# A hybrid decoder block on one core: two groups of GpSimd subtractions and additions are done on VectorE

## The chip, the cores and the metric

The kernel runs on one core of one Trainium2 chip. Its time is in device microseconds (us), as the median of several executions; smaller is better. A core has five engines that work side by side, each through its own queue in a fixed order: TensorE (PE: matmuls, with its weight loads shown as PEld), VectorE (DVE), ScalarE (ACT), GpSimd (POOL) and SyncE (SP, which here only issues DMAs). They wait for each other by semaphores.

## The reference

One decoder layer over a sequence of 2048 positions, 1024 wide, in float32. A conditioning vector c gives shifts, scales and gates (by a product with `ada_w`). Three groups of mixers share one input projection and one output projection:

```
h = rmsnorm(x, norm1_g) * (1 + sc1) + sh1
p = h @ w_in
y = concat[rglru(p), hgrn2(p), rwkv7(p)] * mix_beta
x = x + g1 * (y @ w_out)
h = rmsnorm(x, norm2_g) * (1 + sc2) + sh2
x = x + g2 * ((silu(h @ w_gate) * (h @ w_up)) @ w_down)
return rmsnorm(x, final_g)
```

RG-LRU and its convolution are scans over time, HGRN-2 a gated linear recurrence worked in chunks of 64, RWKV-7 a delta-rule recurrence. The FFN is 2816 wide.

## The kernel before

Everything lies transposed: channels on the 128 partitions, time along the free dimension. Time is cut into four blocks of 512 (`NB`, `TB`), so a tile is 128x512; the 1024 channels are eight tiles (`KC`).

**Split products.** The large ("dense") products keep float32 accuracy with three passes over split numbers: each operand is a high part (rounded by ACT to the narrower type `R`) and a low part (the rest, by a subtraction). `project` (the line L271 in the profile) issues hi·hi, hi·lo and lo·hi into a PSUM bank `pd`, of which there are three. Weights come through `raw_w` into `wr` (three buffers), are split into `wh` and `wl` (four buffers each), and activations into `hh` and `hl` (sixteen each). There are two helpers for the split of an activation: `split_v`, whose subtraction is on VectorE, and `split`, whose subtraction is on GpSimd (L240).

**Stages.** First the shifts and scales, the norm of block 0, then `w_in` products for two blocks at a time, whose results go to DRAM (`pd`). The mixers read them back (`load_p`), work tile by tile, and store `y` to DRAM (`yd`). When a block's mixers are done, `load_y(b)` reads its eight y tiles into `xs` tiles (12 buffers, shared with the residual x and others), splits each with `split`, and `w_out_products` and `ffn` follow. `load_y` of the next block is called inside `ffn`, ahead of the last group of `w_down` products. So there are four places where `split` works: ahead of blocks 0, 1, 2 and 3. I call them the boundaries.

**Squares of a norm.** `square_sum` adds up the squares of eight x tiles: ACT squares, and the sums are made on VectorE, except where the caller gives tiles of its own (`tile`): that is the norm of block 1, worked out ahead in the start of the kernel with `tr` and `th` tiles, whose six additions are on GpSimd (L344). After `rstd_of` its result waits for `norm1(1)`.

**Mixers beside dense work.** The mixers are generators (`mixers_a`: RWKV; `mixers_b`: HGRN and RG-LRU), stepped by `tick` from within `project`, and so their instructions are mixed into those of the dense products. The names to know: `hgrn` works on `th` tiles, multiplies them on VectorE in six levels (blocks of 1, 2, 4, 8, 16, 32 positions), with products on PE between them into the bank `ph`. Those of the last two levels are the small products of 16x16 and 32x32, which the profile names `ph<-th 64*16` and `64*32`. The VectorE products on `big` tiles (128x126, 128x119 and so on) belong to the mixers' work as well.

**What sets the order.** The program is written through a framework that builds each engine's queue: it takes the instructions that are ready in a model of the run, in which each instruction has an assumed duration, and among those the one with the lowest number. `level` gives the numbers: `out` before `load` (weights), `feed` (activations, and what this change touches), `mix` (mixers), `dense` (matmuls). The order that comes out is fixed; at run time an engine never takes a later instruction first. A helper class `Counted` wraps VectorE and ScalarE, so that nearly all of their instructions have one line in the profile, L69; tile names tell them apart.

Of the kernel before, what the change touches and what calls it, by code (L numbers as in the profile page):

```python
# [10 lines left out]
F = mybir.dt.float32  # L11
# [63 lines left out]
def hybrid_kernel(ctx, tc, x, par, ada_w, w_in, rgw, igw, w_up, a_up, g_up, w_out,  # L75
                  w_gate, w_upf, w_down, cst, msk, out):
    nc = tc.nc
    G, PE, SP = nc.gpsimd, nc.tensor, nc.sync
    V, A = Counted(nc.vector, 0.16, 960.0), Counted(nc.scalar, 0.2, 1200.0)
# [21 lines left out]
    def act(o, i, f=AF.Copy, **k):  # L101
        return A.activation(o, i, f, **k)
# [35 lines left out]
    def parts_():  # L138
        return dp.tile([128, TB], R, name="hh", bufs=16), dp.tile([128, TB], R, name="hl", bufs=16)
# [95 lines left out]
                               lambda: bank("pd", 3), xs_)  # L235


    def split(src, hi, lo):
        act(hi, src)
        G.tensor_sub(lo, src, hi.bitcast(F))  # L240

    def split_v(src, hi, lo):
        i = act(hi, src)
        V.tensor_sub(lo, src, hi.bitcast(F))
        return i
# [48 lines left out]
    def finish(b):  # L294
        for s in streams:
            while s["block"] <= b:
                step(s)
# [39 lines left out]
    def square_sum(s, t, k, tile=None, n=1):  # L337

        s, *last = s or (None,)
        if len(last) == n:  # L340
            if s is None:
                s = last.pop(0)
            else:
                (G if tile else V).tensor_add(s, s, last.pop(0))  # L344
        q = (tile or xs_)()
        if k == KC - 1:
            V.tensor_mul(q, t, t)
        else:
            squared[:] = [act(q, t, AF.Square)]
        return s, *last, q  # L350
# [18 lines left out]
    def load_x(src, b, k, tile=None):  # L369
        t = (tile or xs_)()  # L370
        load(t, src[k, :, b * TB:(b + 1) * TB])
        return t

    def x_stats(bs, step, xtile=None, qtile=None, parts=None):
        for b in bs:
            s = None
            for k in range(KC):
                with level("feed"):
                    t = load_x(x, b, k, xtile)
                    if xtile is not None:  # L380
                        X[b, k] = t
                    s = square_sum(s, t, k, qtile)
                if k % step == step - 1:
                    yield
            with level("feed"):
                RS[b] = rstd_of(s, parts)
# [31 lines left out]
    with level("feed"):  # L418
        xsum = None
        xt = [load_x(x, 0, k) for k in range(KC)]  # L420
        w_after[:] = last_load
        tiles = {}
        for k in range(KC):
            for part, tile in ((1, tr_), (0, th_)):
                tiles[part, 0, k] = ada_tile(tile(), part, 0, k)
        for k in range(KC):
            for part, tag in ((1, "hh"), (0, "hl")):
                tiles[part, 1, k] = ada_tile(dp.tile([128, TB], F, name=tag, bufs=16), part, 1, k)
        for k in range(KC):
            xsum = square_sum(xsum, xt[k], k)  # L430
        rs = rstd_of(xsum)

        def shift_and_scale(half, pe):
            drain(zip_longest(*(ada(part, half, lambda k, part=part: tiles[part, half, k], pm_, xs_, pe)
                                for part in (1, 0))))

        shift_and_scale(0, (0, 2, 4))
        head = IN_ORDER[:2]
        W = {c: load_w(w_in[c], split_v) for c in head}
        w_after[:] = last_load  # L440
        h0 = make_h(lambda k: xt[k], rs, A1, B1, ks=range(4))
        ahead = x_stats([1], 8, tr_, th_, lambda: (tile_of("th", R)[:, 0:TB], tile_of("th", R)[:, 0:TB]))
        next(ahead)
        shift_and_scale(1, (0, 1))
        h0 += make_h(lambda k: xt[k], rs, A1, B1, ks=range(4, KC))
# [593 lines left out]
    for f in (mixers_a, mixers_b):  # L1039
        s = {"block": 0, "at": 0.0}  # L1040
# [3 lines left out]
    def load_y(b):  # L1044
        finish(b)
        ys = []
        for k in range(KC):
            t = load_x(yd, b, k)
            y = parts_()
            split(t, *y)  # L1050
            ys.append(y)
        return ys

    def w_out_products(b, ys, before):
        x1, s = [], None
        for d in range(KC):
            ws = load_w(w_out[d], split_v)
            t = load_x(x, b, d)
            p, = project(ys, ws)
            with level("out"):  # L1060
                stt(t, p, G1[:, d:d + 1], t, OP.mult, OP.add)
            if d == 0:
                before()
            s = square_sum(s, t, d)
            x1.append(t)
        return x1, rstd_of(s)
# [17 lines left out]
    def ffn(b, x1, rs):  # L1084
        h = make_h(lambda k: x1[k], rs, A2, B2, "silu_and_others", over=False)
        gs, s, ys = [], None, None
        for f0 in range(0, NF, 4):
            n = min(4, NF - f0)
            while len(gs) < min(f0 + n + (2 if f0 + n + 2 >= NF else 1), NF):
                gs.append(ffn_up(h, len(gs)))  # L1090
            if len(gs) == NF and ys is None and b + 1 < NB:
                ys = load_y(b + 1)
            for d in range(KC):
                p, = project(gs[f0:f0 + n], load_w(w_down[d][:, f0 * 128:(f0 + n) * 128], split_v))
                with level("out"):
                    stt(x1[d], p, G2[:, d:d + 1], x1[d], OP.mult, OP.add)
                if f0 + n == NF:
                    s = square_sum(s, x1[d], d, n=1 if b + 1 < NB else 2)

        def final_norm():  # L1100
            rs = rstd_of(s)
            for d in range(KC):
                with level("dense"):
                    stt(x1[d], x1[d], pc("final_g", d), rs, OP.mult, OP.mult)
                    SP.dma_start(out[d, :, b * TB:(b + 1) * TB], x1[d])

        return ys, final_norm
# [22 lines left out]
    with level("feed"):  # L1130
        ys, before = load_y(0), lambda: None
# [60 lines left out]
```

## Time and profile before

| what | value |
|---|---|
| median of 3 runs | 2862.96 us (2861.45 to 2866.43) |
| the profiled execution | 2862.48 us |
| its span, first to last instruction | 2860.7 us |
| mean granted clock of TensorE | 0.983 |
| dense products (L271) | 9696 of 14842 matmuls |
| GpSimd's subtractions (L240) | 32, at 866, 1350, 1895 and 2401 us |
| GpSimd's additions (L344) | 6, at 43 to 58 us |
| GpSimd's other work | memsets, 24 of them of KG tiles (22.7 us) |

How to read the rows of a profile: `out<-in` names the tile written and the tiles read, with buffer numbers left out. In a list of groups there follow the shape, the number of instructions, then busy us and mean ns of one, then how long the engine was idle just before them and for whom it waited. In a timeline a row begins with its start and its length in us; the square bracket at its end is the idle time ahead of it. In a list of waits the numbers are us in total, times, and the longest. Granted clock 1.00 is TensorE's full speed.

### The profile page before, as it was taken

The page shows a single profiled execution, that of the slowest core. Times are in us where ns is not written, and L with a number is a line of the kernel's source. Part 1 is how long each engine was busy: PE and PEld are TensorE (multiplying, and loading weights), DVE is VectorE, ACT ScalarE, POOL GpSimd, SP SyncE. Part 2 cuts the span into 40 slices and gives each one's busy share as a digit, 9 for nine tenths or more (in the row PEclk, how much of TensorE's full clock was granted, in tenths as well). Part 3 has the DMA queues.
Part 4 walks back from the last instruction along what each step waited for, and adds up shares of the span by engine and source line. Part 5 has one row for each costly group of instructions (what it writes and reads, how often), then busy time and mean ns, then how long its engine had stood idle before and what let it go on. Part 6 is the DMA issues. An engine that isn't in the chain of part 4 may idle for free. (4 is left out here: it accounts for less than half of the span.)

```text
span 2860.7 us, 41286 instructions
## 1 busy us (share of the span) xinstructions
PE 2732.2 (96%) x14842; PEld 2196.6 (77%) x14842; DVE 1932.6 (68%) x4112; ACT 1476.4 (52%) x2466; POOL 80.0 (3%) x67
## 2 busy tenths in 40 slices
PE   7999998999998999999989999999999999999998
PEld 6787776777876688877767877877778788788886
DVE  7677667867686875687877858778776445644435
ACT  4433854464547743666477456746773433433333
POOL 2000000000001000001000000010000001000000
PEclk9999999999999999999999999999999999999999
DMA  7553455544444242434333434335233333433332
GB/s 256 186 148 114 137 166 161 160 137 145 128 128 131 93 122 81 141 100 137 108 111 97 122 89 129 113 111 158 75 112 102 93 96 121 145 99 96 97 99 85
DMA packets 242590, 352.27 MB, mean 123 GB/s; under 512 B 72913, under 2 KB 78545, under 8 KB 242385
## 3 DMA queue, kind: packets, MB, share of 16 engines
q1 hardware_dynamic: 160144, 285.55, 31.9%
q10 hardware_dynamic: 82240, 64.09, 8.5%
q8 instruction: 117, 1.92, 0.3%
q14 instruction: 89, 0.72, 0.1%
HBM read 293.92 MB, written 55.62 MB: 122 GB/s over the span
## 5 line engine op out<-in xcount | busy, mean ns | idle before, releaser
L271 PE MATMUL pd<-hh,wh 128*128 128x512 f32 x3232 | 1295.1, 402 | 26.7 <-ACT hh L69 23.2
L271 PE MATMUL pd<-hl,wh 128*128 128x512 f32 x3232 | 1284.6, 398 | 5.0 <-DVE hl L69 3.9
L271 PE MATMUL pd<-hh,wl 128*128 128x512 f32 x3232 | 1282.4, 397 | 1.3 <-DVE wl L69 1.3
L69 ACT ACTIVATE wh<-wr 128x512 fp32r<-128x512 f32 (+1 forms) x752 | 464.0, 620 | 892.8 <-PE pd L271 719.6
L271 PEld LDWEIGHTS pd<-hh,wh 128*128 128x128 f32 x3232 | 613.5, 190 | 154.8 <-ACT hh L69 26.2
L271 PEld LDWEIGHTS pd<-hl,wh 128*128 128x128 f32 x3232 | 613.8, 190 | 136.2 <-DVE hl L69 8.9
L69 DVE TENSOR_TENSOR wl<-wr,wh 128x512 fp32r<-128x512 f32 (+1 forms) x752 | 510.8, 683 | 300.9 <-ACT wh L69 282.0
L271 PEld LDWEIGHTS pd<-hh,wl 128*128 128x128 f32 x3232 | 613.4, 190 | 130.3 <-issue 3.3
L69 ACT ACT_TABLE_LOAD x227 | 291.2, 1283 | 9.1 <-DVE tr L69 2.3
L69 DVE SCALAR_TENSOR_TENSOR xs<-pd,Q,xs 128x512 f32<-128x512 f32 x224 | 167.7, 748 | 141.6 <-PE pd L271 132.8
L69 DVE TENSOR_TENSOR th<-th 128x256 f32<-128x256 f32 (+8 forms) x349 | 155.0, 458 | 29.7 <-ACT th L69 23.3
L69 DVE TENSOR_TENSOR big<-big 128x30 f32<-128x30 f32 (+7 forms) x480 | 117.1, 244 | 10.2
L69 DVE TENSOR_TENSOR xs<-pd,xs 128x512 f32<-128x512 f32 x88 | 60.8, 691 | 87.2 <-PE pd L271 85.3
L69 ACT ACTIVATE xs<-pd 128x512 f32<-128x512 f32 x140 | 82.6, 590 | 69.4 <-PE pd L271 61.5
L69 ACT ACTIVATE th<-th 128x512 f32<-128x512 f32 (+2 forms) x153 | 93.3, 611 | 45.5 <-DVE th L69 25.8
L69 ACT ACTIVATE hh<-xs 128x512 fp32r<-128x512 f32 x120 | 74.4, 628 | 40.4 <-DVE xs L69 24.9
L69 ACT ACTIVATE hw<-big,we 64x64 f32<-64x64 f32 x192 | 66.1, 344 | 46.0 <-DVE big L69 43.1
L69 ACT ACTIVATE tr<-tr 128x512 fp32r<-128x512 f32 (+4 forms) x112 | 69.2, 626 | 13.9 <-DVE tr L69 12.9
L240 POOL TENSOR_TENSOR hl<-xs,hh 128x512 fp32r<-128x512 f32 x32 | 43.2, 1377 | 989.2 <-ACT hh L69 987.5
L69 DVE SCALAR_TENSOR_TENSOR big<-pc,we,hw 64x64 f32<-64x64 f32 x168 | 47.4, 282 | 32.5 <-PE pc L302 28.6
L69 DVE TENSOR_TENSOR tr<-tr 128x512 fp32r<-128x512 f32 (+2 forms) x80 | 54.7, 686 | 18.3 <-ACT tr L69 17.8
L69 DVE TENSOR_TENSOR hl<-xs,hh 128x512 fp32r<-128x512 f32 x88 | 60.7, 689 | 6.2 <-ACT hh L69 2.0
(185 smaller groups left out, 2290.7 us busy)
## 6 DMA issues: line engine op xcount, KB each, us to landing
wr<-in_w_gate SPq DMA_DIRECT2D x176, 256.0 KB, 2.6
wr<-in_w_upf SPq DMA_DIRECT2D x176, 256.0 KB, 2.6
wr<-in_w_down SPq DMA_DIRECT2D x160, 256.0 KB, 2.7
wr<-in_w_in SPq DMA_DIRECT2D x144, 256.0 KB, 3.4
pd<-xs SPq DMA_DIRECT2D x108, 256.0 KB, 3.1
xs<-in_x SPq DMA_DIRECT2D x72, 256.0 KB, 4.2
wr<-in_ada_w SPq DMA_DIRECT2D x64, 256.0 KB, 3.3
th<-pd ACTq DMA_DIRECT2D x64, 256.0 KB, 3.5
```

The source lines that it names most:

```text
L69: return f(*a, **k)
L240: G.tensor_sub(lo, src, hi.bitcast(F))
L271: PE.matmul(p, a[:, c], b, start=(n == 0), stop=(n == tot - 1))
```

## The change

The subtraction of `load_y` and the additions in block 1's sum of squares go from GpSimd to VectorE. `split` has no other user and is removed.

```
-    def split(src, hi, lo):
-        act(hi, src)
-        G.tensor_sub(lo, src, hi.bitcast(F))
-
     def split_v(src, hi, lo):
         i = act(hi, src)
         V.tensor_sub(lo, src, hi.bitcast(F))
...
             if s is None:
                 s = last.pop(0)
             else:
-                (G if tile else V).tensor_add(s, s, last.pop(0))
+                V.tensor_add(s, s, last.pop(0))
...
             t = load_x(yd, b, k)
             y = parts_()
-            split(t, *y)
+            split_v(t, *y)
             ys.append(y)
```

Since the queues are built by a model of the run, the order of the other instructions changes as well. GpSimd is left with memsets. VectorE's queue in the start, around the last four x tiles of block 0 (`xs<-xs,Q,rstd` is the norm, `hl<-xs,Q,hh` the low part that PE waits for, `th<-th` an addition of squares), before:

```order
L69 SCALAR_TENSOR_TENSOR xs<-xs,Q,rstd 128x512 x3
L69 TENSOR_TENSOR wl<-wr,wh 128x512 x2
L69 SCALAR_TENSOR_TENSOR xs<-xs,Q,rstd 128x512
L69 COPY tr<-pcar 128x1
L69 SCALAR_TENSOR_TENSOR hl<-xs,Q,hh 128x512 x3
L69 TENSOR_TENSOR th<-tr 128x512
L69 SCALAR_TENSOR_TENSOR hl<-xs,Q,hh 128x512
```

and now:

```order
L69 SCALAR_TENSOR_TENSOR xs<-xs,Q,rstd 128x512 x3
L69 TENSOR_TENSOR wl<-wr,wh 128x512 x2
L69 TENSOR_TENSOR th<-th 128x512
L69 SCALAR_TENSOR_TENSOR xs<-xs,Q,rstd 128x512
L69 TENSOR_TENSOR th<-th 128x512
L69 SCALAR_TENSOR_TENSOR hl<-xs,Q,hh 128x512
L69 TENSOR_TENSOR th<-th 128x512
L69 SCALAR_TENSOR_TENSOR hl<-xs,Q,hh 128x512
L69 TENSOR_TENSOR th<-th 128x512
L69 TENSOR_TENSOR th<-tr 128x512
L69 TENSOR_TENSOR th<-th 128x512
L69 SCALAR_TENSOR_TENSOR hl<-xs,Q,hh 128x512
```

The additions now stand between the low parts: two of them are ahead of the first.

VectorE's queue at the boundary of block 1, around the last `w_down` products of block 0's FFN (`xs<-pd,Q,xs` adds a product to the residual and frees its bank, `wl<-wr,wh` is a weight's low part, `hl<-xs,hh` a subtraction: the first one is the FFN's own, the others are y's; `big` is mixers' work), before:

```order
L69 TENSOR_TENSOR hl<-xs,hh 128x512
L69 TENSOR_TENSOR big<-big 128x6x19
L69 COPY_PREDICATED big<-M,ph 64x32x8
L69 SCALAR_TENSOR_TENSOR xs<-pd,Q_79,xs 128x512
L69 TENSOR_TENSOR big<-big 128x126
L69 TENSOR_TENSOR wl<-wr,wh 128x512
L69 TENSOR_TENSOR big<-big 128x7x18
L69 TENSOR_TENSOR th<-th 128x32x8
L69 TENSOR_TENSOR big<-big 128x119
```

and now:

```order
L69 TENSOR_TENSOR hl<-xs,hh 128x512 x2
L69 SCALAR_TENSOR_TENSOR xs<-pd,Q_79,xs 128x512
L69 TENSOR_TENSOR hl<-xs,hh 128x512
L69 TENSOR_TENSOR wl<-wr,wh 128x512
L69 TENSOR_TENSOR hl<-xs,hh 128x512
L69 TENSOR_TENSOR big<-big 128x6x19
L69 SCALAR_TENSOR_TENSOR xs<-pd,Q_79,xs 128x512
L69 TENSOR_TENSOR wl<-wr,wh 128x512
L69 TENSOR_TENSOR hl<-xs,hh 128x512 x3
L69 SCALAR_TENSOR_TENSOR xs<-pd,Q_79,xs 128x512
L69 TENSOR_TENSOR wl<-wr,wh 128x512
L69 TENSOR_TENSOR hl<-xs,hh 128x512
```

The eight subtractions of y stand among the weights and the residual's additions, and the mixers' `big` and `th` work that was there stands behind them. On PE the products of that work are later by as much: counted in dense products (L271), HGRN's 16x16 step stands 40 later than before and its 32x32 step 33. At the boundary of block 2 the same happens, by 59 and 56 products.

More of the change, by code (lines that the diff above doesn't have):

```diff
@@ L235, in ada_rest @@
                                lambda: bank("pd", 3), xs_)
-    def split(src, hi, lo):
-        act(hi, src)
-        G.tensor_sub(lo, src, hi.bitcast(F))
     def split_v(src, hi, lo):
@@ L343, in square_sum @@
             else:
-                (G if tile else V).tensor_add(s, s, last.pop(0))
+                V.tensor_add(s, s, last.pop(0))
         q = (tile or xs_)()
@@ L1049, in load_y @@
             y = parts_()
-            split(t, *y)
+            split_v(t, *y)
             ys.append(y)
```

## The prediction

> **What bounds the kernel now.** I read the page's head first: how long, and which engine is full.
>
> ```profile
> span 2860.7 us, 41286 instructions
> PE 2732.2 (96%) x14842; PEld 2196.6 (77%) x14842; DVE 1932.6 (68%) x4112; ACT 1476.4 (52%) x2466; POOL 80.0 (3%) x67
> ```
>
> TensorE is the bound: 96% of the span is matmul work that the change leaves alone. Only the other 128.5 us (2860.7 - 2732.2), in which PE idles, can move, and the work that PE does at a reduced clock. A time saved on VectorE (DVE) or GpSimd (POOL) counts only where PE waits for it. So I read next what POOL does and what the same operation costs on DVE, in the view that groups instructions by line (busy us, then mean ns of one).
>
> ```profile
> L240 POOL TENSOR_TENSOR hl<-xs,hh 128x512 fp32r<-128x512 f32 x32 | 43.2, 1377 | 989.2 <-ACT hh L69 987.5 <-DMA xs<-yd 0.8 <-PE pd L271 0.7
> L344 POOL TENSOR_TENSOR th<-th 128x512 f32<-128x512 f32 x6 | 10.3, 1720 | 39.5 <-DMA tr<-in_x 34.6 <-ACT th L69 4.5
> L69 DVE TENSOR_TENSOR hl<-xs,hh 128x512 fp32r<-128x512 f32 x88 | 60.7, 689 | 6.2 <-ACT hh L69 2.0
> L69 DVE TENSOR_TENSOR th<-th 128x512 f32<-128x512 f32 x64 | 43.9, 688 | 16.6 <-ACT th L69 15.9
> ```
>
> The 38 instructions take 53.5 us on POOL. On DVE they cost 38 x 0.69 = 26.2 us: about half each, but on an engine that is 68% busy instead of 3%.
>
> Next, how busy the engines are in the stretches in which POOL does them (columns: stretch, length, then busy us of PE, PEld, DVE, ACT, POOL, then the granted clock).
>
> ```profile
> 49.82:58.03 8.21, 5.69 (x13) 4.05 (x14) 8.21 (x7) 4.39 (x8) 7.89 (x5) 0.58 0.75 223
> 866.45:876.86 10.41, 9.39 (x43) 7.26 (x43) 3.83 (x8) 9.25 (x21) 10.41 (x8) 0.84 0.50 187
> 1349.82:1362.82 13.00, 9.78 (x104) 7.54 (x102) 12.61 (x19) 6.26 (x11) 10.60 (x8) 1.00 0.51 147
> 1894.98:1906.65 11.67, 5.81 (x54) 4.63 (x52) 11.42 (x18) 5.12 (x9) 10.72 (x8) 0.90 0.52 158
> ```
>
> In the start and at the boundaries of blocks 1 and 2, DVE is full while POOL works, and PE is not: 5.81 of 11.67 us in the last row. What fills DVE there? Grouping DVE's instructions in the block 1 stretch, the block 2 stretch, and a stretch just ahead of the first, in that order:
>
> ```profile
> L69 DVE TENSOR_TENSOR wl<-wr,wh 128x512 fp32r<-128x512 f32 x2 | 2.8, 1379 | 0.0
> L69 DVE TENSOR_TENSOR big<-big 128x126 f32<-128x126 f32 x3 | 2.6, 875 | 0.0
> L69 DVE TENSOR_TENSOR big<-big 128x119 f32<-128x119 f32 x2 | 2.6, 1305 | 0.0
> L69 DVE TENSOR_TENSOR big<-big 128x128 f32<-128x128 f32 x2 | 1.6, 823 | 0.1
> L69 DVE SCALAR_TENSOR_TENSOR xs<-pd,Q,xs 128x512 f32<-128x512 f32 x2 | 1.5, 752 | 0.2
> ...
> L69 DVE TENSOR_TENSOR wl<-wr,wh 128x512 fp32r<-128x512 f32 x2 | 2.3, 1150 | 0.0
> L69 DVE TENSOR_TENSOR big<-big 128x128 f32<-128x128 f32 x2 | 2.3, 1136 | 0.0
> L69 DVE TENSOR_TENSOR big<-big 128x119 f32<-128x119 f32 x2 | 2.0, 992 | 0.0
> L69 DVE TENSOR_TENSOR th<-th 128x256 f32<-128x256 f32 x2 | 1.9, 945 | 0.0
> L69 DVE TENSOR_TENSOR big<-big 128x126 f32<-128x126 f32 x2 | 1.2, 615 | 0.0
> ...
> L69 DVE TENSOR_TENSOR wl<-wr,wh 128x512 fp32r<-128x512 f32 x5 | 3.4, 689 | 1.0 <-ACT wh L69 1.0
> L69 DVE TENSOR_TENSOR th<-th 128x256 f32<-128x256 f32 x10 | 4.1, 416 | 0.0
> L69 DVE TENSOR_TENSOR big<-big 128x120 f32<-128x120 f32 x2 | 0.6, 284 | 0.0
> ```
>
> The same instructions last two to four and a half times as long while POOL works. It hits those with two operands in SBUF; the one that reads a PSUM bank (xs<-pd) keeps its 0.75 us. DVE is not short of work capacity there: part of its "busy" time is being held by POOL. Against the third group (big taken at 0.28), block 1 loses 2 x 0.69 + 3 x 0.59 + 2 x 1.02 + 2 x 0.54 = 6.3 us, block 2 2 x 0.46 + 2 x 0.85 + 2 x 0.71 + 2 x 0.53 + 2 x 0.33 = 5.8 us. The start shows it too, on the instructions that PE needs first (one, then three, of a kind that takes 0.75):
>
> ```profile
> 50.07 1.75 DVE L69 SCALAR_TENSOR_TENSOR xs<-xs,Q,rstd 128x512 f32<-128x512 f32 x1
> 51.81 5.08 DVE L69 SCALAR_TENSOR_TENSOR hl<-xs,Q,hh 128x512 fp32r<-128x512 f32 x3
> ```
>
> **What PE pays for it.** PE's rows at those places, with the idle time ahead of each and its releaser, and the list of waits:
>
> ```profile
> 53.56 0.80 PE L271 MATMUL pd<-hl,wh 128*128 128x512 f32 x1 [0.96 <-DVE hl L69]
> 1354.98 0.68 PE L302 MATMUL ph<-th 64*16 64x16 f32 x64 [2.19 <-DVE th L69]
> 1366.38 1.06 PE L302 MATMUL ph<-th 64*32 64x32 f32 x32 [4.60 <-DVE th L69]
> 1905.55 1.07 PE L302 MATMUL ph<-th 64*32 64x32 f32 x32 [5.86 <-DVE th L69]
> PE pd L271 <- POOL hl L240: 1.1, 2, 0.7
> ```
>
> POOL itself holds PE for 1.1 us only. Its larger price goes by way of DVE: HGRN's chain on big and th is late, and PE, whose order is fixed, stands at the product that needs it. After the two long waits PE also runs slowly (first and last slow product after each; then an undisturbed stretch of the chain of waits):
>
> ```profile
> 1367.96 0.63 PE L271 MATMUL pd<-hl,wh 128*128 128x512 f32 x1
> 1371.37 0.57 PE L271 MATMUL pd<-hh,wh 128*128 128x512 f32 x1
> 1907.14 0.63 PE L271 MATMUL pd<-hh,wh 128*128 128x512 f32 x1
> 1910.55 0.63 PE L271 MATMUL pd<-hh,wl 128*128 128x512 f32 x1
> 2240.50 195.88 PE pd L271 x864
> ```
>
> Eight products lie between each pair: 3.41 / 8 = 0.426 us each, against 195.88 / 864 = 0.227. That is 8 x 0.20 = 1.6 us lost after each long wait, 3.2 in all.
>
> **The change, part by part.**
>
> *The subtractions at the boundaries of blocks 1 and 2.* Eight subtractions cost DVE 8 x 0.69 = 5.5 us; the stretching that ends gives back 6.3 and 5.8. For DVE it is a draw. But in the new order PE's products have moved: counting PE's dense products (L271) in it, the 16x16 step of HGRN stands 40 of them later than before in block 1 and 59 in block 2, the 32x32 step 33 and 56 later. The order now counts those subtractions on DVE, while the old one knew nothing of DVE being held. At 0.227 us the slack is 9.1 and 7.5 us in block 1, 13.4 and 12.7 in block 2.
>
> What could eat it: DVE keeps its order, and a subtraction that waits for its y tile holds the queue. Before, only ScalarE (ACT) waited for those tiles:
>
> ```profile
> ACT hh L69 <- DMA xs<-yd: 14.3, 12, 2.6
> SPq L164 <- POOL hl L240: 8.6, 10, 0.9
> ```
>
> That is 14.3 / 4 = 3.6 us a boundary. Bounds for what DVE will wait: 0, since the loads themselves waited 8.6 us for POOL to free a tile, which DVE does in half the time, and 3.6. At 3.6 the chain is later by 5.5 - 6.3 + 3.6 = 2.8 us in block 1 and by 5.5 - 5.8 + 3.6 = 3.3 in block 2. The waits would then be 2.19 + 2.8 - 9.1, 4.60 + 2.8 - 7.5 and 5.86 + 3.3 - 12.7: all at or below zero. So I take all three as gone: **-12.7 us** (2.19 + 4.60 + 5.86), and the slow clock with them, **-3.2 us**. What is late next there is nothing of this chain; it is ACT's weights, whose waits are for PE.
>
> *Block 0's boundary.* DVE is busy 3.83 of 10.41 us; eight subtractions of 0.69 fit in the gaps. PE's 1.1 us of waits on POOL go: **-1.1** (bounds 0 and -1.1). *Block 3's boundary:* nothing, since PE is full and DVE has room:
>
> ```profile
> 2401.26:2412.79 11.53, 11.53 (x52) 9.55 (x52) 7.85 (x9) 6.23 (x12) 11.49 (x8) 1.00 0.56 173
> ```
>
> *The six additions of block 1's squares, in the start.* They stand in DVE's queue between the last xs and the hl that PE waits for: two of them ahead of the first hl. From 50.07: 0.69 + 0.75 + 0.69 + 0.75 ends near 52.95; before, 1.75 and a third of 5.08 end near 53.5. So **-0.5** (bounds: -0.96, the whole wait, and +0.8, if the end of the stretching gives nothing on these).
>
> *The rest of the order.* From about 1350 us to the last mixer's work, PE, DVE and ACT get a different order, the mixers' products mostly 10 to 80 dense products later. No dense product waits for those mixers soon; but the new order has waits of its own. I bound them by 0 and by all that I took off, 17.5. The nearest row is the stretch between the two boundaries:
>
> ```profile
> 1370.00:1893.00 523.00, 508.88 (x2885) 403.63 (x2888) 395.40 (x880) 325.72 (x540) 5.68 (x6) 0.99 0.39 114
> ```
>
> PE idles 14.1 us there. I take half of that as new waits: **+7** (a choice).
>
> **Sum.** -12.7 - 3.2 - 1.1 - 0.5 + 7 = -10.5. The profiled execution took 2862.48 us (1.8 more than its span), the median is 2862.96; so 2852.0 against the one and 2852.5 against the other. I say 2852.
>
> **Rivals.**
>
> *Given back.* The mixers' order is new over 800 us, and every wait removed comes back elsewhere: the 14.1 us of idle above shows that such waits are common outside the POOL stretches too. Then 2862 +- 5. For it: DVE's own balance is a draw (+26.2, less some 16 of stretching). Against: the three waits lie right in the POOL stretches or behind them.
>
> *The queue behind a late y tile (slower).* DVE holds at a subtraction; behind it stand the low parts of weights (wl) and the additions that free PSUM banks; PE stops. Price: ACT's 14.3 us go to PE in full, the old waits stay, less 1.6 for block 0 and the start: 2862.5 + 14.3 - 1.6 = 2875. It decides when one wait outlasts the weights prepared ahead.
>
> ```profile
> ACT wh L69 <- PE pd L271: 719.6, 426, 10.0
> ```
>
> Against it: ACT mostly waits for PE to free a weight tile, up to 10.0 us, so weights are ahead by far more than the longest single wait, 2.6.
>
> *DVE becomes the bound.* If the long instructions above were long for another reason, the 12.61 of 13.00 and 11.42 of 11.67 us stay and 5.5 us come on top in each of the two stretches: 2862.5 + 11.0 = 2873.5. It decides if wl still takes over 1 us there. Against it: the rows ahead of the stretch, and xs<-pd, unchanged inside it. [...]
>
> That the change doesn't do what it says can be left out: POOL's new order holds memsets alone.
>
> **Chances.** Forecast 0.60; given back 0.25; the late tile 0.09; DVE the bound 0.06. About 0.2%, 5.7 us, is what a measurement of this kernel can tell from no change. So faster 0.60, same 0.25, slower 0.15. Range: at the low end the sum with no new waits gives 2845, and 2842 leaves room for a better order; at the high end it takes in all of "given back" and goes to 2869; the two slow cases and a little of the low end are left out.
>
> **What would show it.** Right: wl and big near 0.69 and 0.28 us at the boundaries; no PE wait over 1 us on th at the 16x16 and 32x32 steps of blocks 1 and 2; DVE busy some 5 to 10 us more in all. Wrong: DVE's hl waiting on ACT's hh for several us at a boundary with PE idle behind it; or PE's idle total still near 128.5 us, with new waits on DVE between 1370 and 2240 us.

## The result, and the profile after

The changed kernel took 2846.66 us (median of 6 runs, 2840.93 to 2848.35), the kernel before beside it 2862.53 (6 runs, 2860.56 to 2866.43): ratio 0.9939, 95% interval 0.9926 to 0.9951, so 0.5 to 0.7% faster. The forecast was 2852, with a range from 2842 to 2869.

The head of the page after, and PE's row:

```profile
span 2840.7 us, 41245 instructions
PE 2724.8 (96%) x14842; PEld 2188.8 (77%) x14842; DVE 1934.6 (68%) x4150; ACT 1472.7 (52%) x2464; POOL 26.5 (1%) x29
```

Two differences are to be seen. PE's idle time is the span less PE's busy time: 115.9 us now, 128.5 before, so 12.6 less. And DVE, which got 38 instructions more (26.2 us at 0.69), is busy only 2.0 us longer: some 24 us of what it did before was being held.

In the changed kernel's rows `project` is L267 and the helper of the mixers' products L298; before, they were L271 and L302. DVE's groups in 1346 to 1363 us, the new place of block 1's boundary (busy us, mean ns, idle before):

```profile
L69 DVE TENSOR_TENSOR hl<-xs,hh 128x512 fp32r<-128x512 f32 x9 | 6.0, 685 | 1.2 <-ACT hh L69 1.2
...
L69 DVE TENSOR_TENSOR wl<-wr,wh 128x512 fp32r<-128x512 f32 x4 | 2.7, 685 | 0.5 <-ACT wh L69 0.5
...
L69 DVE TENSOR_TENSOR big<-big 128x126 f32<-128x126 f32 x2 | 0.6, 283 | 0.0
...
L69 DVE TENSOR_TENSOR big<-big 128x119 f32<-128x119 f32 x2 | 0.5, 270 | 0.0
```

`wl` is at 685 ns, where it was 1379, and `big` at 283 and 270, where it was 875 and 1305. The eight subtractions are there and cost 0.69 each. PE's rows at the 16x16 and 32x32 steps of HGRN, block 1 and then block 2, in its timeline:

```profile
1360.37 0.68 PE L298 MATMUL ph<-th 64*16 64x16 f32 x64 [1.67 <-DVE th L69]
...
1366.17 0.70 PE L298 MATMUL ph<-th 64*32 64x32 f32 x32 [0.57 <-DVE th L69]
...
1893.85 0.68 PE L298 MATMUL ph<-th 64*16 64x16 f32 x64 [1.70 <-DVE th L69]
```

Block 1's waits of 2.19 and 4.60 us have become 1.67 and 0.57. Block 2's wait of 5.86 us, at the 32x32 step, is gone, and its 16x16 step, for which PE did not wait before, now has one of 1.70. At these steps PE idled 12.65 us before and 3.94 now: 8.7 less, beside 12.6 in the whole run. Another 4.1 went at a place that the prediction does not name, the second norm of block 1. The rows there, of before:

```profile
1468.41 0.95 PE L302 MATMUL pc<-rs,GIQ 128*128 128x64 f32 x4
1474.55 1.22 PE L271 MATMUL pd<-hh,wh 128*128 128x512 f32 x2 [5.19 <-ACT hh L69]
```

and of after:

```profile
1446.68 0.49 PE L298 MATMUL pm<-KG,big 128*128 128x128 f32 x2
1447.46 1.13 PE L298 MATMUL ph<-th,rgt 128*128 128x512 f32 x2 [0.29 <-DVE th L69]
1448.42 0.61 PE L298 MATMUL pc<-big,KG 128*128 128x128 f32 x4
1448.87 0.39 PE L298 MATMUL pm<-KG,big 128*128 128x128 f32 x2
1449.83 0.66 PE L298 MATMUL pc<-rs,GIQ 128*128 128x64 f32 x4 [0.58 <-ACT rs L69]
1451.53 0.73 PE L267 MATMUL pd<-hh,wh 128*128 128x512 f32 x2 [1.04 <-ACT hh L69]
```

While the norm is worked out, no dense product can go. Before, one group of mixers' products stood in that pause and PE idled 5.19 us. In the new order mixers' work of RG-LRU and RWKV, which is later now, fills it, and 1.04 us are left. The second norm of block 0 gained in like manner: its waits of 1.26, 2.09 and 2.99 us (946 to 954 us) became 0.81 and 3.29 (940 to 946 us), 2.2 us less.

New waits did come. The largest, in the list of PE's waits before and after:

```profile
PE pm L302 <- DVE tr L69: 8.7, 10, 5.1
...
PE pm L298 <- DVE tr L69: 14.4, 11, 6.6
```

The longest of these is at 118 us, in the start. Two more of over 1.5 us stand where PE did not wait before, 1.57 us at 974.72 and 1.66 us at 1943.18. DVE's and ACT's waits for the y tiles, DVE's before and then both after:

```profile
DVE hl L69 <- ACT hh L69: 2.0, 4, 1.1
...
DVE hl L69 <- ACT hh L69: 10.1, 18, 1.9
ACT hh L69 <- DMA xs<-yd: 14.1, 11, 2.2
```

ACT waits for y as before (14.3). DVE, whose order now has these subtractions, waits 10.1 us for ACT instead of 2.0, and none longer than 1.9.

### The profile page after: what moved, and what is told of

The parts are those of the page before. It is cut to its first block, busy times and chain, and to the rows that moved or that the text cites. A ratio compares the mean times of both kernels' runs of the same rounds, so it can differ in the third digit from the quotient of the medians.

```text
span 2840.7 us, 41245 instructions
## 1 busy us (share of the span) xinstructions
PE 2724.8 (96%) x14842; PEld 2188.8 (77%) x14842; DVE 1934.6 (68%) x4150; ACT 1472.7 (52%) x2464; POOL 26.5 (1%) x29
## 5 line engine op out<-in xcount | busy, mean ns | idle before, releaser
L267 PE MATMUL pd<-hh,wh 128*128 128x512 f32 x3232 | 1289.5, 400 | 20.6 <-ACT hh L69 19.2
L267 PE MATMUL pd<-hl,wh 128*128 128x512 f32 x3232 | 1280.8, 396 | 3.8 <-DVE hl L69 3.7
L267 PE MATMUL pd<-hh,wl 128*128 128x512 f32 x3232 | 1281.9, 397 | 0.0
L267 PEld LDWEIGHTS pd<-hh,wh 128*128 128x128 f32 x3232 | 612.2, 190 | 150.0 <-ACT hh L69 21.9
L267 PEld LDWEIGHTS pd<-hl,wh 128*128 128x128 f32 x3232 | 612.3, 189 | 133.8 <-DVE hl L69 9.1
L267 PEld LDWEIGHTS pd<-hh,wl 128*128 128x128 f32 x3232 | 611.8, 189 | 127.9 <-issue 3.4
L69 DVE TENSOR_TENSOR wl<-wr,wh 128x512 fp32r<-128x512 f32 (+1 forms) x752 | 504.2, 674 | 301.1 <-ACT wh L69 284.2
L69 DVE TENSOR_TENSOR th<-th 128x256 f32<-128x256 f32 (+7 forms) x355 | 158.0, 458 | 26.8 <-ACT th L69 23.4
L69 DVE TENSOR_TENSOR big<-big 128x30 f32<-128x30 f32 (+7 forms) x480 | 108.2, 225 | 10.1 <-DMA big<-nd 0.2
L69 DVE TENSOR_TENSOR hl<-xs,hh 128x512 fp32r<-128x512 f32 x120 | 81.7, 688 | 14.1 <-ACT hh L69 9.8
L69 ACT ACTIVATE xs<-xs 128x512 f32<-128x512 f32 x77 | 48.1, 627 | 43.6 <-DVE xs L69 40.1
```

What stands on the lines that cost most here:

```text
L69: return f(*a, **k)
L267: PE.matmul(p, a[:, c], b, start=(n == 0), stop=(n == tot - 1))
```

## The experiments

**Theory.** GpSimd's subtractions read two operands from SBUF, and DVE's instructions with two operands in SBUF are held meanwhile (before, `wl` took 1379 ns beside them in block 1, 689 just ahead). Their end brings the gain. **Rivals:** the new order of the mixers brings it; a busy GpSimd costs by itself, or the tiles that it frees late; the additions in the start bring a part. Medians come with their interval against the kernel before on the same chip; the last column is span less PE busy, from one profile each.

| kernel | median us | ratio, 95% interval | PE idle us |
|---|---|---|---|
| before | 2862.53 | | 128.5 |
| after | 2846.66 | 0.9939 [0.9926, 0.9951] | 115.9 |
| subtractions only (e1) | 2846.12 | 0.9949 [0.9933, 0.9966] | 114.5 |
| additions only (e2) | 2862.97 | 1.0009 [1.0000, 1.0018] | 126.5 |
| after, short GpSimd reads (e3) | 2846.92 | 0.9950 [0.9938, 0.9961] | 116.3 |
| before, no reads (e4) | 2846.00 | 0.9950 [0.9939, 0.9962] | 114.2 |
| after, full GpSimd reads (e5) | 2848.65 | 0.9968 [0.9956, 0.9980] | 113.8 |
| before, writes only (e6) | 2847.01 | 0.9953 [0.9940, 0.9967] | 114.6 |
| before, one operand read (e7) | 2846.59 | 0.9960 [0.9947, 0.9973] | 115.0 |
| after once more (e8) | 2848.04 | 0.9953 [0.9941, 0.9966] | 116.0 |
| full GpSimd reads once more (e9) | 2850.12 | 0.9966 [0.9953, 0.9978] | 116.9 |
| after, double GpSimd reads (e10) | 2872.38 | 1.0041 [1.0027, 1.0055] | 129.5 |

The kernel before had medians of 2862.53 (beside after), 2861.33 (e1 to e4), 2857.91 (e5 to e7) and 2860.97 us (e8 to e10), so ratios are compared, or runs of one chip.

### Which of the two edits

Subtractions moved, additions left on GpSimd (e1), and the reverse (e2), against the kernel before:

```
e1:
-            split(t, *y)
+            split_v(t, *y)
e2:
-                (G if tile else V).tensor_add(s, s, last.pop(0))
+                V.tensor_add(s, s, last.pop(0))
```

> Only the 32 subtractions of y go to VectorE; the six additions of squares stay on GpSimd. All engines' orders are those of the changed kernel except in the first 160 us. Theory A (the gain is at the boundaries): 2847 to 2849 us, that is 14 to 16 us below the kernel before; the start keeps its 0.5 to 1 us. Rival (a good part of the gain comes from the start, by way of an earlier norm of block 1): at least 4 us above the changed kernel, 2851 or more.

> Only the six additions go to VectorE; the subtractions stay on GpSimd. All orders are those of the kernel before except in the first 160 us. Theory A: 0 to 1 us below the kernel before (2861.5 to 2862.5), all of it in the start; the three waits at the boundaries (2.2, 4.6, 5.9 us) stay. Rival: 4 us or more below.

The subtractions alone give the gain. The additions give none: the median was 1.6 us above the kernel before, where 0 to 1 below was expected, with an interval that begins at 1.0000. They do what was foreseen locally. DVE's rows in the start, of the additions-only kernel:

```profile
51.12 0.75 DVE L69 SCALAR_TENSOR_TENSOR hl<-xs,Q,hh 128x512 fp32r<-128x512 f32 x1
51.78 0.69 DVE L69 TENSOR_TENSOR th<-th 128x512 f32<-128x512 f32 x1
52.38 0.76 DVE L69 SCALAR_TENSOR_TENSOR hl<-xs,Q,hh 128x512 fp32r<-128x512 f32 x1
```

`hl` is back at 0.75 from 1.69 (5.08 / 3). But PE's next stop, the `tr` product, is reached earlier and waited for longer, 6.34 us against 5.08:

```profile
117.86 1.22 PE L302 MATMUL pm<-tr,bones 128*128 128x512 f32 x2 [6.34 <-DVE tr L69]
```

### Is it the reads, or the new order?

In the old order, GpSimd's subtraction gave way to a memset (e4; the low parts of y are left out, as zero):

```
-        G.tensor_sub(lo, src, hi.bitcast(F))
+        G.memset(lo.bitcast(F), 0.0)
```

> The kernel before, in which GpSimd writes zeros into the low parts of y in place of the subtraction (the low parts of y are left out of the result). It reads nothing. All orders at the boundaries of blocks 1, 2 and 3 are exactly those of the kernel before; around block 0's boundary they differ a little. Theory A: wl and big last 0.69 and 0.28 us at those boundaries and the waits of 2.2, 4.6 and 5.9 us shrink to under 1 us each: 12 to 16 us below the kernel before, 2847 to 2851. Rival (the new order alone): within 3 us of the kernel before.

0.9950: the old order (a little changed around block 0's boundary), without the reads and with no subtraction of y anywhere, is as fast as the new one. But the memsets do not wait for y and went far ahead (1276 to 1340 us for block 1), so GpSimd stood idle at the boundary, and a busy GpSimd was not yet excluded. Two more variants of that line settled it: three memsets, two of them on the xs tile behind ScalarE's read (e6, low parts of y as zero), and a copy of the high part (e7, low parts of y equal to the high ones):

```
e6:
-        G.tensor_sub(lo, src, hi.bitcast(F))
+        G.memset(lo.bitcast(F), 0.0)
+        G.memset(src, 0.0)
+        G.memset(src, 0.0)
e7:
-        G.tensor_sub(lo, src, hi.bitcast(F))
+        G.tensor_copy(lo, hi.bitcast(F))
```

> The kernel before, with GpSimd's subtraction replaced by three memsets of 128x512 (one of the low part, two of the xs tile after ScalarE has read it): y's low parts are left out as zero. GpSimd is then busy at the boundaries for about as long as before and holds the xs tiles as before, but reads nothing. Theory of the reads: wl 0.69 and big 0.28 us at the boundaries, the waits of 2.19, 4.60 and 5.86 us gone or under 1.6, time 2846 +- 3, as in the run without reads. Rival (a busy GpSimd, or tiles that it frees late, are what costs): 2858 to 2863, with PE's waits as before.

> The kernel before, with GpSimd's subtraction replaced by a copy of the high part (one operand read instead of two; y's low parts are then a copy of the high ones, so the result differs). The order of every engine is that of before. If VectorE is held by any GpSimd instruction that reads SBUF, for as long as it lasts: wl and big are stretched beside the copies, and the time lies between 2846 and 2862 by the length of the copy (2856 if it takes three quarters of 1377 ns). If only an instruction with two operands in SBUF holds it: wl 0.69, big 0.28, time 2846 +- 3. If GpSimd being busy is what costs: 2858 to 2862 whatever VectorE's rows show.

At block 1's boundary the write-only kernel has GpSimd busy for 10.54 of 13 us, as before (10.60 of 13), with DVE's groups behind it (window: stretch, length, busy PE, PEld, DVE, ACT, POOL, clock):

```profile
1342.00:1355.00 13.00, 12.02 (x142) 9.50 (x142) 12.06 (x34) 6.82 (x13) 10.54 (x22) 1.00 0.52 163
```

```profile
L69 DVE TENSOR_TENSOR wl<-wr,wh 128x512 fp32r<-128x512 f32 x4 | 2.7, 683 | 0.4 <-ACT wh L69 0.4
L69 DVE TENSOR_TENSOR big<-big 128x126 f32<-128x126 f32 x4 | 1.1, 281 | 0.0
```

No stretching, PE busy 12.02 of the 13 us instead of 9.78, and 0.9953 in time. The 16x16 steps have no wait, and the 32x32 steps of blocks 1 and 2 keep 0.98 and 0.48 of their 4.60 and 5.86 us (the mixers' products are L304 here):

```profile
1353.42 0.69 PE L304 MATMUL ph<-th 64*32 64x32 f32 x32 [0.98 <-DVE th L69]
...
1884.68 0.69 PE L304 MATMUL ph<-th 64*32 64x32 f32 x32 [0.48 <-DVE th L69]
```

So GpSimd's being busy costs nothing here, nor does its holding of the xs tiles; its reading does: `wl` took 1379 ns beside 10.60 us of its subtractions, and 683 ns beside 10.54 us of its writes.

The one-operand kernel has the order of before on every engine, row by row, which makes it the cleanest comparison. GpSimd's copies over the whole run:

```profile
L240 POOL CAST hl<-hh 128x512 fp32r<-128x512 f32 x32 | 20.3, 650 | 1005.7 <-ACT hh L69 1002.2 <-PE pd L271 2.6 <-PE pc L302 1.0
```

They read for 20.3 us instead of 43.2, and DVE is nearly free of them (`wl` at 684 and 733 ns at the two boundaries; beside a copy some `big` of 0.54 to 0.69 and a `wl` of 0.85). PE's rows at the steps that waited 2.19, 4.60 and 5.86 us:

```profile
1348.82 0.68 PE L302 MATMUL ph<-th 64*16 64x16 f32 x64 [0.32 <-DVE th L69]
...
1357.81 0.70 PE L302 MATMUL ph<-th 64*32 64x32 f32 x32 [2.19 <-DVE th L69]
...
1888.83 0.69 PE L302 MATMUL ph<-th 64*32 64x32 f32 x32 [0.58 <-DVE th L69]
```

With not one instruction moved, these waits fall from 12.65 to 3.09 us, the time by 0.4% (0.9960), and DVE is busy 1917.5 us instead of 1932.6. For the old order the theory is thereby shown: what GpSimd's instruction reads is the cause, and no reordering is needed to get the gain. Of this one run it can't be told whether the shorter time or the single operand matters more; that a copy holds DVE at all, the 0.85 shows.

### How much of it does the new order hide?

To the changed kernel, reads on GpSimd were added without use for their result: four of 64 columns into a scratch tile per y tile (e3), one over the full tile (e5, and e9 on the chip of the changed kernel's own second run, e8), two full ones (e10).

```
e3:
+    scratch = cp.tile([128, 64], F, name="scratch")
...
+            h3 = y[0].bitcast(F)
+            for n in range(0, 256, 64):
+                G.tensor_sub(scratch, h3[:, n:n + 64], h3[:, n:n + 64])
e5, e9 (e10 has the line twice):
+            G.tensor_sub(t, y[0].bitcast(F), y[0].bitcast(F))
```

> The changed kernel, with GpSimd kept busy beside VectorE's subtractions of y: four subtractions of 64 columns for each y tile, of the high part from itself, into a scratch tile that nobody reads. The order on all other engines is exactly that of the changed kernel. Theory A (GpSimd's reads hold VectorE's instructions with two operands in SBUF): wl and big at the boundaries of blocks 1 and 2 last well over 0.69 and 0.28 us again; the changed kernel's 16x16 steps already wait 1.7 us there, so PE's waits grow by 3 to 6 us at each of the two: 6 to 13 us above the changed kernel, 2853 to 2860. Rival (the new order alone brings the gain): within 2 us of the changed kernel.

> The changed kernel, with one more instruction per y tile: GpSimd subtracts the high part from itself over the full 128x512, into the xs tile, which nothing reads afterwards. So GpSimd again reads two operands at the boundaries for as long as before the change, while VectorE makes the real low parts in the new order. Theory of the reads: wl and big at the boundaries of blocks 1 and 2 go back to 1.1 to 1.4 and 0.6 to 1.3 us, 6 us of VectorE's time are lost at each, PE's waits at the 16x16 and 32x32 steps grow from 1.7 us to 4 or more, and the time is 2852 to 2862. Theory of the order (the new places of HGRN's steps are what gains): the stretching comes back on VectorE, but the slack of 7 to 13 us takes it, and the time stays at 2847 +- 2.

> The changed kernel itself, to stand beside the two runs below on one chip, since the kernel before alone differed by 4.6 us between chips. Expected ratio to before: 0.992 to 0.996.

> The kernel of the run with full GpSimd reads in the new order, on the same chip as the changed kernel. Its VectorE was busy 11 us longer, PE 4.9 us longer, and PE's waits at the two 16x16 steps grew by 1.3 and 2.4 us. Theory of the reads: 2 to 6 us above the changed kernel. Theory of the order (its slack takes all): within 1.5 us of it.

> As the run above, with two reading subtractions on GpSimd per y tile instead of one, so GpSimd reads at each boundary for some 20 us. Theory of the reads: VectorE's stretching at the boundaries doubles (some 20 us over the changed kernel in all), it goes past the slack, and the time is 6 to 15 us above the changed kernel. Theory of the order: within 2 us of the run with one.

The short reads missed: they kept GpSimd busy, but DVE's rows at block 1's boundary moved little, and the time not at all.

```profile
L69 DVE TENSOR_TENSOR hl<-xs,hh 128x512 fp32r<-128x512 f32 x9 | 6.7, 758 | 0.6 <-ACT hh L69 0.6
...
L69 DVE TENSOR_TENSOR wl<-wr,wh 128x512 fp32r<-128x512 f32 x5 | 3.5, 701 | 0.4 <-ACT wh L69 0.4
```

That run was too weak to tell the theories apart. The full reads (e5) do stretch DVE again, in 1881 to 1897 us:

```profile
L69 DVE TENSOR_TENSOR wl<-wr,wh 128x512 fp32r<-128x512 f32 x4 | 4.2, 1040 | 0.3 <-ACT wh L69 0.3
L69 DVE TENSOR_TENSOR big<-big 128x119 f32<-128x119 f32 x2 | 2.2, 1113 | 0.0
```

and PE's wait at block 2's 16x16 step grows from 1.70 to 4.07 us:

```profile
1896.70 0.72 PE L298 MATMUL ph<-th 64*16 64x16 f32 x64 [4.07 <-DVE th L69]
```

DVE is busy 11 us longer in all (1945.6). Yet the time hardly moves: 2850.12 beside 2848.04 on one chip (e9 and e8), with overlapping intervals. That is at the foot of the 2 to 6 us expected of the reads, and the 5 to 15 us expected before it were too many. The dose is smaller than the old one: 11 us of DVE's time, where the kernel before has some 16.6 more than the write-only e6 (1932.6 less 1916.0). So the new order takes nearly all of this dose; whether it would take the old one, no run shows. Two doses show where the slack ends. DVE's timeline at block 1's boundary in e10, and PE's row behind it:

```profile
1363.19 0.94 DVE L69 TENSOR_TENSOR wl<-wr,wh 128x512 fp32r<-128x512 f32 x1
1364.05 2.97 DVE L69 TENSOR_TENSOR hl<-xs,hh 128x512 fp32r<-128x512 f32 x2
1366.94 1.12 DVE L69 TENSOR_TENSOR big<-big 128x126 f32<-128x126 f32 x1
1367.98 0.74 DVE L69 SCALAR_TENSOR_TENSOR xs<-pd,Q,xs 128x512 f32<-128x512 f32 x1
1368.65 0.94 DVE L69 TENSOR_TENSOR wl<-wr,wh 128x512 fp32r<-128x512 f32 x1
1369.51 1.52 DVE L69 TENSOR_TENSOR hl<-xs,hh 128x512 fp32r<-128x512 f32 x1
```

```profile
1373.58 0.72 PE L298 MATMUL ph<-th 64*16 64x16 f32 x64 [9.23 <-DVE th L69]
```

No row of DVE there has an idle time ahead of it: it is full, `wl`, `hl` and `big`, with two operands in SBUF, are long, and `xs<-pd`, which takes one from PSUM, keeps its 0.74. PE waits 9.23 us. DVE's busy time is 33 us above the changed kernel's, and the run 24.3 us above it on the same chip, slower than the kernel before and more than the 6 to 15 that I expected: past the slack, what holds DVE holds PE. (GpSimd also holds the xs tiles for longer in e10, and the orders of e5 and e10 differ from the changed kernel's in places; but DVE did not wait, so the stretching is what is late.)

## Why the prediction was right, point by point

- **The mechanism** (DVE's two-operand instructions are held while GpSimd works, PE pays by way of HGRN's chain): right, and shown by e7, which shortens the reads and moves nothing, and by e6, which takes them away (its order differs from that of before in places). By the rows of the prediction the instructions last 1.7 (`wl`, 1150 against 689 ns) to 4.6 times as long, a little more widely spread than "two to four and a half". The sum of the stretching was too low. The "some 16" us are the 6.3 and 5.8 of two boundaries and close to 4 of the start, and DVE was to be busy 5 to 10 us longer; it was 2.0, so some 24 came back. About 16.6 of them belong to the subtractions (e6, above) and 6.2 to the additions (in e2 DVE is busy 2.1 us less with 4.1 us of additions on top). The boundaries of blocks 0 and 3, left out of the 16, were stretched too: at block 3 four `wl` took 1.37 us each.
- **-12.7 for the three waits:** -8.7. They shrank, but 1.67 us stayed at block 1's 16x16 step and 1.70 came at block 2's, where I had written that no wait over 1 us would remain. The step that failed is DVE's side of the slack. I let HGRN's chain on DVE be later by 2.8 us at most (the eight subtractions, less the stretching, and a late y tile). The traces show 8.5 at block 1: from the start of the 4201st dense product (1337.99 us before, 1334.89 after) to the end of the `th` product that PE's 16x16 step needs, 16.85 us passed before and 25.33 after. In that stretch DVE now has not only eight more `hl`, but three more `wl` and three more `xs<-pd`, some 4.3 us that the new queue puts ahead of the chain and that I left out, and only a part of the 6.3 us of stretching lay there. With 9.1 us of slack, 2.19 + 8.5 - 9.1 = 1.6 us remain, which is the wait.
- **-3.2 for the slow clock:** half of it at most at these two places. Behind the 1.67 us wait the products stand 0.23 apart; behind that of 1.70 seven are still slow, first and last in the timeline after, (1897.90 - 1895.34) / 6 = 0.427 apart:

```profile
1895.34 0.63 PE L267 MATMUL pd<-hh,wl 128*128 128x512 f32 x1
...
1897.90 0.63 PE L267 MATMUL pd<-hh,wl 128*128 128x512 f32 x1
```

  The granted clock was 1.00 in 1361 to 1364 us and 0.50 in 1895.34 to 1898.33 us, as it was before behind the two long waits (0.50 in 1366.30 to 1371.40 and in 1905.50 to 1911.00 us). In the whole run the term can't be seen. The medians differ by 15.9 us, 3.3 more than the idle time, and PE's busy time differs by 8.6 us between two executions of the changed kernel alone (2724.8 and 2733.4, against 2732.2 before).

- **-1.1 at block 0's boundary:** PE's wait for POOL's `hl` is gone from the list, as foreseen.
- **-0.5 for the additions in the start:** PE's wait for `hl` went from 0.96 to 0.64, and the next wait took it back. By e2 the edit is worth nothing.
- **+7 for new waits, "a choice":** mis-sized, and the main reason why the forecast was 5 us short. The gains named above make 8.7 + 4.1 + 2.2 + 1.1 + 0.3 = 16.4 us of idle time; 12.6 were measured in all, so the rest of the program gave back about 3.8 on balance; the new waits at 118, 975 and 1943 us alone make 1.5 + 1.6 + 1.7 = 4.8. I had bounded the effect of the new order on one side only, by nothing and a loss; it also had gains to give, 4.1 and 2.2 us in the pauses of two norms, that nearly outweigh my 7. That the forecast of 2852 came within 5.4 us of the measured 2846.66 is in part luck: the 4.0 us too many at the three waits stood against these.
- **"Given back":** not here, though it is what happened to the additions. **The late y tile:** ACT's 14.1 us of waiting for y stayed where it was, and DVE's longest wait for it was 1.9 us. **DVE the bound:** not with the change; but e10 shows that this rival is a real one, 24 us dear, as soon as GpSimd reads for twice as long.

Two roads led to the same time. In the old order the low parts without reads (e4, e6, e7) reach 114 to 115 us of PE idle and keep the 5 us pause at block 1's norm; the changed kernel has 116, with that pause filled but waits of 1.7 us at the 16x16 steps. And the new order with reads on GpSimd (e5, e9) is still 0.3% faster than before (0.9968 and 0.9966). So each of the two brings most of the gain without the other (the new order with the smaller dose of e9: 2850.12 us, where the kernel before had 2860.97 and the changed one 2848.04 on that chip), and they do not add up. How much of the changed kernel's 16 us is due to its order alone can't be told: no run has the reads gone, the subtractions on DVE and the old order.

## What to carry to other kernels

An engine that was 3% busy slowed a fuller one here: GpSimd's subtractions took 43.2 us in all, and `wl` on VectorE took 1379 ns beside them in block 1, 689 just ahead. So look at the mean length of the same instruction inside and outside the stretches where a second engine works, and by where its operands lie. Work with two operands in SBUF that was given to GpSimd beside such work on VectorE saved little here, since VectorE lost much of what it saved (15.1 us, by e7, of 32 x 0.69 = 22.1, and all of it where it was full: 6.3 and 5.8 us lost at the boundaries of blocks 1 and 2, for 5.5 saved at each); work that only wrote cost nothing (e6: `wl` 683 ns beside 10.54 us of it). And where a framework builds the queues, a new order can have gains as well as waits to give (here 4.1 and 2.2 us in the pauses of two norms, against 4.8 of new waits): bound it from both sides.

## What the runs showed of the hardware

- The hold does not go with the time that GpSimd is busy: beside full subtractions (1.33 us each) `wl` rose to 1.04 us (e5) and `hl` to 1.49 (e10), beside those of 64 columns (0.47 us each, e3) `hl` rose only from 685 to 758 ns and `wl` from 685 to 701, though these made GpSimd busy for 59.6 us in all and e5's for 41.9. The short ones also read half as many columns, so whether the length of an instruction or the amount that it reads decides, these runs can't tell.
- GpSimd seems to be held as well. In the kernel before, its subtraction took 1.28 to 1.30 us in the three that had no instruction of VectorE beside them (866.45, 867.69 and 2408.48 us), and 1.62 to 1.75 in the five that began beside the rest of a `wl` (875.13, 1900.44, 2403.77, 2406.77 and 2411.04 us). Its copies in e7 took 0.62 us in the mean at block 0's boundary, where VectorE was busy for 3.83 of 10.41 us before, and 0.67 at block 1's, where it was for 12.61 of 13.00.
- PE's slow clock did not go by the length of the wait alone: 1.70 us and, in the second run of the same kernel, 1.57 us were followed by slow products at block 2, 1.67 and 1.35 us at block 1 were not. The granted clock fell with them: it was 0.50 behind the 1.70 us and 1.00 behind the 1.67. What sets it, no run shows.
- PE's busy time is not a property of the kernel alone: it was 2724.8 and 2733.4 us in two profiled executions of the changed kernel, while the idle time was 115.9 and 116.0. For a small change, the idle time was the steadier measure of the two.
